# Recurrent layer: score products on quarters of the array, and 32-row corrections issued in turn with the masked values

## The chip, the cores and the metric

The kernel runs on one core of a Trainium2 chip. The metric is the device time of one execution in microseconds (us), from three runs of the kernel before: 1291.12, 1292.26 and 1293.33, with a median of 1292.26.

The engines of the core are named as in the profile: PE is the matrix engine (TensorE), with PEld for its loads of stationary operands; DVE is VectorE, ACT is ScalarE, POOL is GpSimd and SP the engine that issues most DMAs. A matrix product holds one operand in the array (the stationary one, rows by columns) and streams the other through it (the moving one); its result goes to PSUM, from where ACT or DVE copies it on.

## The reference

The model is a two-layer trunk over 512 tokens of width 1024. Layer 0 mixes time with an RWKV-7 recurrence (12 heads of width 64) beside attention into 256 memory tokens; layer 1 uses chunked attention. Each layer ends with a gated feed-forward. All arithmetic is float32. The change touches the recurrence alone:

```python
def step(state, inp):
    r_t, w_t, k_t, v_t, a_t, b_t = inp
    sa = jnp.einsum('bhvk,bhk->bhv', state, a_t)
    state = (state * w_t[:, :, None, :] + sa[..., None] * b_t[:, :, None, :]
             + v_t[..., None] * k_t[:, :, None, :])
    return state, jnp.einsum('bhvk,bhk->bhv', state, r_t)
```

The state of a head is 64 x 64. It decays channel by channel, takes a rank-one correction (a, b) and a rank-one update (v, k), and is read with r. 512 such steps are computed for each head.

## The kernel before, in words

The 512 tokens are cut into 8 chunks of 64 (`NCH`), and two heads share one tile of 128 partitions: head h = 0 lies in partitions 0 to 63 (`HS[0]`), head h = 1 in 64 to 127 (`HS[1]`). So there are six head pairs (`NPAIR`). Inside a chunk the recurrence is solved in closed form: with scores between the tokens of a chunk, the inverse of a unit triangular 64 x 64 matrix, and products with it; only the state passes from chunk to chunk.

Each pair goes through three generators. `prepare` (L1126) makes the projections, the decays and keys, the first scores, and solves the 16 x 16 diagonal blocks of the inverse with DVE and some DMAs. `front` (L1290) computes the score products (L1300), masks them into the tile `ML` on DVE (L1303), transposes keys and values (L1314, L1324, L1326), and builds the 32 x 32 blocks of the inverse from 16 x 16 ones (L1358, L1375). `back` (L1400) completes the inverse to 64 x 64 and runs the chunks.

The change touches these places:

- In `front`, for each half of the chunks (`c4`), two PSUM tiles take the scores, one per head. For each chunk and head one product has a stationary operand of 64 x 128 (two of the three 64-wide slots of `KB`) and 128 moving columns (`AR`). Each head uses its 64 array rows and all 128 array columns.
- In `back`, the first 16 products (L1410) begin the correction that joins two 32-row blocks of the inverse: 32 x 32 stationary, 32 moving columns, at array rows `h*64` to `h*64+32` and array columns `h*64+32` to `h*64+64`. ACT copies them to `X5` (L1414). The second step of the correction (L1424) uses `X5` and finishes `Tt`.
- Between those two, 16 products (L1418) multiply the masked scores with the values: 64 x 64 stationary, 64 moving columns, array rows of the other head (`HS[1 - h]`) and array columns of the own head (`HS[h]`). ACT copies them to `VT[:, 2]` (L1419). Then L1434 applies the inverse to what both steps have made.

The order of the work is written by a planner, `weave` (L87). Each generator yields an estimated cost in nanoseconds, and, as a second number, a time that must pass in the plan before it is asked again; the planner always asks the ready generator with the least share of its total done (`BACK_COST` and its like are these totals). In one stage it weaves `back` of one pair, `front` of the next and `prepare` of the one after (L1577 to L1581); the last stage holds the backs of the last two pairs, one `front` and the memory attention (L1609). These numbers make no semaphores; the build derives the waits from the data and can exchange products whose inputs come ready at other times. The scores, the corrections and the values all take PSUM tiles from one pool of four (`S=4`).

## Time and profile before

| what | us |
|---|---|
| timed runs | 1291.12, 1292.26, 1293.33 |
| median | 1292.26 |
| span of the profiled execution, first to last instruction | 1292.6 |
| PE busy in it | 1260.9 (98%) |
| DVE busy | 1031.7 (80%) |
| ACT busy | 846.4 (65%) |
| DMA packets, bytes | 95581, 192.14 MB |

The profile comes from one execution apart from the timed ones; its span is the time that it gives.

How to read the rows that follow. A row of the timeline gives the start and the duration in us, the engine, the line of the kernel, the operation, the tile written and those read, the stationary shape (rows\*columns), the moving shape, and how many records in sequence were merged (x16); in square brackets stands idle time just before, and what ended it. A float32 product leaves two records. The end of a matrix product is modelled, and products overlap, so durations of PE rows can't be added; the distance between two starts can. In the view of one line, the three durations are the least, the median and the greatest in ns. In the view by windows, each row gives a stretch of the span, the busy time of an engine in it with its count of records, and the granted clock of the matrix engine as a share.

### The profile page before, as it was taken

The numbers are of one execution on the slowest core, as the hardware profiler recorded it, in microseconds if no ns is written. First come the engines' busy times: TensorE is split into PE (matmuls) and PEld (weight loads), VectorE is DVE, ScalarE is ACT, GpSimd is POOL, SyncE is SP. The second block draws the span as 40 slices with busy tenths as digits, with TensorE's granted clock in tenths as the row PEclk, the third lists the DMA queues.
The fourth block names the chain that finished last, engine by engine and source line by source line (L and its number), as shares of the span: only waits on it lengthen the run. The fifth ranks groups of instructions, "written<-read, shape, count | busy, mean of one in ns | idle before, by whom it ended". The sixth has DMA issues, their size and how long they took to land.

```text
span 1292.6 us, 26432 instructions
## 1 busy us (share of the span) xinstructions
PE 1260.9 (98%) x10420; PEld 1083.1 (84%) x10420; DVE 1031.7 (80%) x1956; ACT 846.4 (65%) x1398; POOL 152.7 (12%) x182
## 2 busy tenths in 40 slices
PE   9999999999999999999999999999999999999997
PEld 7887777777789999998888878787789999998886
DVE  7867677765688999998876876658889999998684
ACT  6566767856476777776554676757757777765662
POOL 1000000000001222320220000000002222211200
PEclk9999999999999999999999999999999999999999
DMA  5364444453055988996984322234429989978951
GB/s 204 110 174 106 100 96 89 92 109 96 30 166 126 212 198 198 206 208 172 274 185 122 118 87 82 76 104 123 130 61 212 197 193 211 208 161 262 233 149 66
DMA packets 95581, 192.14 MB, mean 149 GB/s; under 512 B 22112, under 2 KB 30432, under 8 KB 95456
## 3 DMA queue, kind: packets, MB, share of 16 engines
q1 hardware_dynamic: 68592, 129.14, 31.9%
q0 software_dynamic: 26864, 61.31, 27.3%
q8 instruction: 82, 1.34, 0.4%
q14 instruction: 43, 0.35, 0.1%
HBM read 174.20 MB, written 6.29 MB: 140 GB/s over the span
## 4 chain that ended last, share of the span: by engine, by line
PE 62%; DVE 15%; ACT 8%; DMA 8%; issue 6%; SPq 0%; POOL 0%; ACTq 0%; DVEq 0%; POOLq 0%
PE psf L434 8%; PE psf L698 7%; PE psd L245 6%; PE psd L241 5%; PE psd L242 5%; DMA wlv<-in_ffn_in_dram 4%; PE psf L436 4%; PE psf L703 4%; PE psd L698 3%; ACT whi L499 2%; DMA wraw<-in_ffn_in_dram 2%; PE psd L703 2%; DVE raw L486 1%; PE pss L1817 1%; DVE wlo L504 1%
## 5 line engine op out<-in xcount | busy, mean ns | idle before, releaser
L499 ACT CAST whi<-raw 128x1024 fp32r<-128x1024 f32 (+1 forms) x168 | 153.3, 942 | 62.3 <-PE psf L434 29.5
L434 PE MATMUL psf<-th,whi 128*128 128x256 f32 x672 | 161.4, 278 | 2.5 <-ACT tmp L553 1.9
L434 PE MATMUL psf<-tl,whi 128*128 128x256 f32 x672 | 161.1, 276 | 0.0
L195 ACT CAST whi<-wraw 128x1024 fp32r<-128x1024 f32 x84 | 87.6, 1048 | 78.3 <-PE psd L242 37.4
L434 PEld LDWEIGHTS psf<-th,whi 128*128 128x128 f32 x672 | 125.8, 188 | 3.9 <-ACT tmp L553 2.9
L434 PEld LDWEIGHTS psf<-tl,whi 128*128 128x128 f32 x672 | 126.0, 188 | 0.0
L504 DVE TENSOR_TENSOR wlo<-raw,whi 128x1024 fp32r<-128x1024 f32 (+1 forms) x108 | 109.3, 1012 | 9.1 <-ACT whi L499 8.9
L241 PE MATMUL psd<-r1h,whi 128*128 128x512 f32 x264 | 107.4, 408 | 0.0
L242 PE MATMUL psd<-r1l,whi 128*128 128x512 f32 x264 | 105.0, 398 | 0.0
L203 DVE TENSOR_TENSOR wlo<-wraw,whi 128x1024 fp32r<-128x1024 f32 x65 | 79.2, 1219 | 22.3 <-ACT whi L195 20.4
L688 ACT CAST whi<-raw 128x1024 fp32r<-128x1024 f32 (+1 forms) x52 | 49.6, 954 | 59.9 <-PE psf L698 33.1
L689 DVE TENSOR_TENSOR wlo<-raw,whi 128x1024 fp32r<-128x1024 f32 (+1 forms) x52 | 56.5, 1097 | 38.9 <-ACT whi L688 31.5
L436 PE MATMUL psf<-th,wlo 128*128 128x256 f32 x504 | 78.0, 276 | 0.0
L245 PE MATMUL psd<-r1h,wlo 128*128 128x512 f32 x264 | 74.3, 403 | 0.6 <-DMA wlo<-in_ffn_in_dram 0.4
L471 POOL DMA_DIRECT2D wlv<-in_ffn_in_dram x40 | 60.7, 1516 | 59.5 <-DVE tmp L572 59.1
L436 PEld LDWEIGHTS psf<-th,wlo 128*128 128x128 f32 x504 | 66.8, 188 | 0.0
L434 PE MATMUL psf<-r2h,whi 128*128 128x256 f32 x252 | 60.9, 278 | 0.7 <-ACT whi L499 0.7
L434 PE MATMUL psf<-r1h,whi 128*128 128x256 f32 x252 | 60.7, 277 | 0.7 <-ACT whi L499 0.7
L434 PE MATMUL psf<-r2l,whi 128*128 128x256 f32 x252 | 60.7, 277 | 0.0
L434 PE MATMUL psf<-r1l,whi 128*128 128x256 f32 x252 | 60.6, 277 | 0.0
L241 PEld LDWEIGHTS psd<-r1h,whi 128*128 128x128 f32 x264 | 49.6, 188 | 12.0 <-issue 2.1
L525 ACT ACTIVATE tmp<-tmp,vec 128x512 f32<-128x512 f32 x44 | 36.0, 817 | 33.3 <-DVE tmp L512 33.3
(611 smaller groups left out, 3576.8 us busy)
## 6 DMA issues: line engine op xcount, KB each, us to landing
raw<-in_ffn_in_dram SPq DMA_DIRECT2D x42, 512.0 KB, 5.2
raw<-in_ffn_in_dram SPq DMA_DIRECT2D x84, 256.0 KB, 5.5
wlv<-in_ffn_in_dram POOLq DMA_DIRECT2D x40, 512.0 KB, 8.6
raw<-in_ffn_out_dram SPq DMA_DIRECT2D x30, 512.0 KB, 6.2
raw<-in_ffn_out_dram POOLq DMA_DIRECT2D x24, 512.0 KB, 8.4
wraw<-in_wA_dram SPq DMA_DIRECT2D x20, 512.0 KB, 4.1
wraw<-in_w_out_dram SPq DMA_DIRECT2D x16, 512.0 KB, 4.1
wraw<-in_ffn_outp_dram SPq DMA_DIRECT2D x16, 512.0 KB, 4.5
```

What stands on the lines that cost most here:

```text
L195: high = lambda: pin(SC.copy(hi[:, :n], raw))
L203: pin(V.tensor_tensor(lo[:, :n], raw, hi[:, :n], op=ALU.subtract))
L241: PE.matmul(ps, wh[:, j * P:(j + 1) * P], ah, start=start and n == 0, stop=False)
L242: dense_at[0] = PE.matmul(ps, wh[:, j * P:(j + 1) * P], al, start=False, stop=False)
L245: dense_at[0] = PE.matmul(ps, wl[:, j * P:(j + 1) * P], act(k)[0], start=False, stop=stop and n == len(ks) - 1)
L434: PE.matmul(ps, wh[:, o + k * P:o + k * P + P], x[k][n], start=k == n == 0, stop=False)
L436: PE.matmul(ps, wl[:, ol + k * P:ol + k * P + P], x[k][0], start=False, stop=k == 3)
L471: GP.dma_start(self.low[:].rearrange("p (a s) -> p a s", a=2), self.second, accum_op=ALU.add)
L499: keep(SC.copy(hi[:, :n], self.pair(what) if n > S else self.raw[:, what]))
L504: keep(V.tensor_tensor(lo[:, :n], self.pair(what) if n > S else self.raw[:, what], hi[:, :n], op=ALU.subtract))
L698: PE.matmul(ps[:], a[:, k0 + i, ts], hi[:, i * S:i * S + S], start=bool(first) and (first is True or t in first) and a is act[0] and i == ...
L703: PE.matmul(ps[:], act[0][:, k0 + i, ts], lo[:, i * S:i * S + S], start=False, stop=bool(last) and t in last and i == n - 1)
```

## The change

In `front`, each score product with a 64 x 128 stationary operand becomes two with 64 x 64. The four products of a chunk sit in the four quarters of the array: rows of head h, columns of half n, in the order (0,0), (1,1), (0,1), (1,0). The moving operand and the results stay what they were.

In `back`, the corrections and the values were two blocks, each with a yield of its own. They become one: for each chunk the two corrections and then the two value products. The values have a second PSUM tile, `pz`, taken at the same time. All copies on ACT stand behind the whole block. The two yields (650 and `MC`, which is 1280) become one of `MC` with a wait of 400, and `BACK_COST` loses 650.

```diff
     U = [(c, h, HS[h], HS[1 - h]) for c in range(NCH) for h in range(2)]
+    QUADS = ((0, 0), (1, 1), (0, 1), (1, 0))
     MC = 16 * 80
...
-                for h in range(2):
-                    PE.matmul(ps[h][:, c], KB[HS[h], cc, 1 - h:3 - h].rearrange("p s t -> p (s t)"),
+                for h, n in QUADS:
+                    PE.matmul(ps[h][HS[n], c], KB[HS[h], cc, 1 - h + n],
                               AR[HS[h], cc].rearrange("p s t -> p (s t)"), start=True, stop=True)
...
-        ps = ups()
-        for c, h, ap, vp in U:
-            lo, hi_ = slice(h * 64, h * 64 + 32), slice(h * 64 + 32, h * 64 + 64)
-            PE.matmul(ps[hi_, c, 0:32], ML[lo, h, c, 32:64], Tl[lo, c], start=True, stop=True,
-                      tile_position=(h * 64, h * 64 + 32))
+        ps, pz = ups(), ups()
+        for c in range(NCH):
+            for h in range(2):
+                lo, hi_ = slice(h * 64, h * 64 + 32), slice(h * 64 + 32, h * 64 + 64)
+                PE.matmul(ps[hi_, c, 0:32], ML[lo, h, c, 32:64], Tl[lo, c], start=True, stop=True,
+                          tile_position=(h * 64, h * 64 + 32))
+            for h in range(2):
+                PE.matmul(pz[HS[h], c], ML[HS[1 - h], h, c, 0:64], VT[HS[1 - h], h, c], start=True, stop=True)
         for h in range(2):
             hi_ = slice(h * 64 + 32, h * 64 + 64)
             SC.copy(X5[hi_], ps[hi_, :, 0:32])
-        yield 650
-        ps = ups()
-        for c, h, ap, vp in U:
-            PE.matmul(ps[ap, c], ML[vp, h, c, 0:64], VT[vp, h, c], start=True, stop=True)
-        SC.copy(VT[:, 2], ps[:])
-        yield MC
+        SC.copy(VT[:, 2], pz[:])
+        yield MC, 400
...
-    BACK_COST = 2 * 650 + 2 * MC + 4 * 1100 + 1700 + 6 * 150 + 7 * 150 + 700 + 1080
+    BACK_COST = 650 + 2 * MC + 4 * 1100 + 1700 + 6 * 150 + 7 * 150 + 700 + 1080
```

## The prediction

> **What bounds the kernel now.** I read the page first (engine shares, the chain), then the stage in which the changed lines run, then the TensorE timeline around them.

> ```profile
> span 1292.6 us, 26432 instructions
> PE 1260.9 (98%) x10420; PEld 1083.1 (84%) x10420; DVE 1031.7 (80%) x1956; ACT 846.4 (65%) x1398; POOL 152.7 (12%) x182
> ...
> PE 62%; DVE 15%; ACT 8%; DMA 8%; issue 6%; SPq 0%; POOL 0%; ACTq 0%; DVEq 0%; POOLq 0%
> ```

> The changed lines run from 81 us (first scores) to 317 us (last corrections). Busy time of PE in the windows with the `back` pieces:

> ```profile
> core 0: us, PE busy (x), PEclk, DMA share, GB/s
> 105.00:147.00 42.00, 40.21 (x624) 1.00 0.44 96
> ...
> 306.00:330.00 24.00, 23.81 (x458) 1.00 0.10 31
> sum 225.00, PE 218.74; mean PE 36.46
> ```

> PE is busy 218.74 of 225 us at the full clock. While one head pair's recurrence runs, the dense projections of the next pair fill in, so what PE does longer comes out at the end almost in full. I therefore price everything in PE time, from start to start, because the modelled durations overlap. One whole set of the changed sections, and the number of records:

> ```profile
> 288.63 0.69 PE L1410 MATMUL pss<-Tl,ML 32*32 32x32 f32 x32
> 289.25 1.16 PE L1300 MATMUL pss<-AR,KB 64*128 64x128 f32 x16
> 290.34 1.15 PE L1418 MATMUL pss<-VT,ML 64*64 64x64 f32 x32
> 291.42 0.48 PE L1300 MATMUL pss<-AR,KB 64*128 64x128 f32 x2
> ```
> ```profile
> L1410 PE MATMUL pss<-Tl,ML x160: 191/191/212, 112.3 to 289.1; 32*32 32x32 f32 x160
> L1410 PE MATMUL pss<-AR,ML x32: 191/191/212, 314.3 to 314.8; 32*32 32x32 f32 x32
> ```
> ```profile
> L1300 PE MATMUL pss<-AR,KB x192: 272/272/373, 81.3 to 293.3; 64*128 64x128 f32 x192
> ```

> Each fp32 product leaves two records, so 192 records of L1410 are 16 corrections in each of six backs, and 192 of L1300 are 8 score products in each of twelve half sections. From the starts: corrections 289.25 - 288.63 = 0.62 us, a score half 290.34 - 289.25 = 1.09 us, the masked values 291.42 - 290.34 = 1.08 us.

> These rows also show what happens where the shape of the stationary operand changes. Each section starts 0.07 us before the modelled end of the one ahead of it (288.63 + 0.69 = 289.32 against 289.25; 290.41 against 290.34; 291.49 against 291.42). Where the shape stays, nothing of the kind is seen:

> ```profile
> 215.25 0.23 PE L1326 MATMUL pss<-cst,v 64*64 64x64 f32 x2
> 215.26 0.27 PE L1445 MATMUL pss<-ML,W 64*64 64x128 f32 x1
> ```

> Here another line's product starts 0.01 us after a product that lasts 0.23 us. So the array empties when the tile shape changes and only then.

> **The price of one change of shape.** Two short sections give it.

> ```profile
> 112.28 0.24 PE L1410 MATMUL pss<-Tl,ML 32*32 32x32 f32 x2
> 112.46 0.49 PE L1300 MATMUL pss<-AR,KB 64*128 64x128 f32 x2
> 112.87 0.69 PE L1410 MATMUL pss<-Tl,ML 32*32 32x32 f32 x30
> ```
> ```profile
> 314.00 0.33 PE L1467 MATMUL psl<-W,MQ 64*64 64x64 f32 x4
> 314.27 0.69 PE L1410 MATMUL pss<-AR,ML 32*32 32x32 f32 x32
> ```

> A section with a single correction takes 112.46 - 112.28 = 0.18 us, one with 16 (two quarters at a time, so eight times as long in work) 0.62 us: 0.44/14 = 0.031 us for each of its 2 or 16 passes, and 0.12 us fixed. A section with one 64x64 product in each of two quarters, as L1467 is, takes 0.27 us, one with eight in each 1.08 us: 0.81/14 = 0.058 us a pass and 0.15 us fixed. The fixed part is the emptying and the slower first pass.

> **The change part by part.**

> Corrections in turn with values. Per chunk the new loop issues two 32x32 corrections, then two 64x64 products, so PE goes through eight sections of each kind where it had one. The work stays; the fixed parts come seven times more: 7 x (0.12 + 0.15) = 1.90 us a back (8 x 0.45 = 3.60 instead of 0.62 + 1.08 = 1.70). Six backs: +11.4 us. The open point is whether the shapes drain each other even where they use different quarters: correction h sits in the quarter (rows h, columns h), value product h in (rows 1-h, columns h). The trace never has this pair. Its nearest row is the 112.87 one above: the score product at 112.46 is the first of half h = 0, in array rows 0 to 63; of the 30 correction records behind it 16 belong to half 1, in rows 64 to 95, and none started before 112.87, 0.08 us before that product's modelled end. Their input was there:

> ```profile
> 111.39 0.89 DVE L1405 STREAM_TRANSPOSE Tl<-Tt 32x256 f32<-32x256 f32 x2
> ```

> Both transposes had ended at 112.28. So disjoint rows don't spare the wait (the columns were shared), and I take the full price; the other bound is that corrections vanish under the values, -0.62 us a back. [...]

> Shapes that now match. After the last value product the 64x64 scores follow with no change of shape in five backs (L1300 stood behind L1410 in each, as at 289.25): one fixed part less, 5 x 0.15 = -0.75 us. A second score half stands directly ahead of L1434, also 64x64, in three:

> ```profile
> 165.80 1.16 PE L1300 MATMUL pss<-AR,KB 64*128 64x128 f32 x16
> 166.89 1.96 PE L1434 MATMUL pss<-VT,Tt 64*64 64x128 f32 x32
> 168.78 0.50 PE L242 MATMUL psd<-r1l,whi 128*128 128x512 f32 x1
> ```

> 3 x 0.15 = -0.45 us, if the order stays.

> Scores by quarters. The number of products doubles, each with half the columns of weights and the same 128 moving columns. Two rows bound it:

> ```profile
> 300.00 1.09 PE L1445 MATMUL pss<-ML,W 64*64 64x128 f32 x16
> 301.02 0.50 PE L241 MATMUL psd<-r1h,whi 128*128 128x512 f32 x1
> ```
> ```profile
> 91.25 0.27 PE L1324 MATMUL pss<-cst,AR 64*64 64x64 f32 x2
> 91.27 0.28 PE L1326 MATMUL pss<-cst,v 64*64 64x64 f32 x2
> ...
> 92.35 0.50 PE L241 MATMUL psd<-r1h,whi 128*128 128x512 f32 x1
> ```

> Eight products of the new shape in two quarters take 1.02 us (L1445). Four quarters cost hardly more than two: L1324 and L1326 put 64 records of 64 columns into 92.35 - 91.25 = 1.10 us, where L1418's 32 in two quarters took 1.08. So 1.04 us a half instead of 1.09: 12 x -0.05 = -0.6 us. Bounds: nothing gained, or the quarters not overlapping at all, as 16 products two at a time do in L1434 (168.78 - 166.89 = 1.89 us): +0.8 us a half. The rows are nearest to the first. The masking on DVE (L1303) and all copies keep count and size; no DMA is added.

> What waits move. Two PSUM tiles of the four in that pool are now taken together, and the copies of the corrections start only when all 16 are done:

> ```profile
> 113.60 0.74 ACT L1414 COPY X<-pss 32x256 f32<-32x256 f32 x2 [0.24 <-PE pss L1410]
> ...
> 116.94 0.58 ACT L1419 COPY VT<-pss 128x512 f32<-128x512 f32 x1
> ```

> That is 1.3 us of ACT copies behind the section, ahead of L1424, which needs the first 0.74. The scores (1.04) and the dense products that the plan puts between cover it; without them each back would lose 0.74 us. Against that, PE waits near these places today:

> ```profile
> 119.87 0.29 PE L1434 MATMUL pss<-VT,Tt 64*64 64x128 f32 x1 [0.63 <-ACT Tt L1428]
> ...
> 164.09 1.15 PE L1418 MATMUL pss<-VT,ML 64*64 64x64 f32 x32 [0.65 <-DVE ML L1303]
> ...
> 201.58 1.56 PE L1300 MATMUL pss<-AR,KB 64*128 64x128 f32 x16
> ...
> 240.75 1.71 PE L1300 MATMUL pss<-AR,KB 64*128 64x128 f32 x16
> ```

> 0.63, 0.65 and the two stretched score halves (1.56 and 1.71 against 1.16, 0.40 and 0.55) make 2.2 us, and a slower section ahead gives the other engines time to catch up. I let half of it go: -1.1 us. The plan itself (one yield of 650 less, a wait of 400 more, both numbers of the planner and no semaphores) reorders a few dense products; I take 0, between -2.2 (all those waits gone) and one wait like 0.65 more in each of six stages, +3.9.

> Sum: 11.4 - 0.75 - 0.45 - 0.6 - 1.1 = +8.5 us. The profiled execution's span, 1292.6, is 0.3 above the median of 1292.26 and within the runs (1291.12 to 1293.33); I add to the median: **1300.8 us**.

> **The rivals.**

> A, the forecast: every chunk drains twice. From 8.5 with the bounds of the waits (-1.1 to +3.9, and these seldom in full): 1297.5 to 1304.

> B, faster: products in wholly separate quarters don't drain each other, so the corrections run under the values. Place: the new loop; it decides if a correction and a value product of different shape overlap at all. It gains 6 x 0.62 = 3.7, and the -1.8 of the other parts: about 1286.8. For it: same-shape products in four quarters do run together (L1324 with L1326). Against it: every change of shape quoted drains, also across rows. [...]

> C, no change that can be told: the order that the build finally gives PE groups the two kinds, since products are taken as their inputs come ready (the lone score product at 112.46 slipped in between that way). With few alternations left only the -1.8 us remains: 1290.5. Against it: in the other backs the corrections stand in one block, as written.

> D, the change doesn't do what it says for the scores: quarters with 128 moving columns don't overlap. 12 x 0.8 = 9.6 in place of -0.6, on top of A: 1311. L1324 and L1326 speak against it.

> **How the numbers follow.** A 0.66, B 0.22, C 0.08, D 0.04. A's own range is 1297.5 to 1304; to leave out no more than 2 in 10 the range goes down over C to about the middle of B's cases, 1287 to 1304.5. This kernel's measurement can tell about 0.2% (2.6 us) from no change. Faster: nearly all of B, 0.20. Within: C, a B that hides little, 0.12. Slower: A and D less a small tail, 0.68.

> **What would show it.** Right: in the timeline the corrections and values stand in eight alternating groups, x4 each, about 0.45 us a chunk and 3.6 us a back, each starting some 0.07 us before the modelled end of the one ahead; score halves of 32 records take about 1.04 us. B would show correction records starting within a value product's duration, and the two kinds through in about 1.1 us. C would show long blocks of one kind. D would show a score half near 1.9 us. The forecast fails if a back's section is under 2 us, or if the stage's PE wait falls by more than the 2.2 us counted.

## The result, and the profile after

The changed kernel takes 1309.64 us in the median of four executions, against 1292.61 for the kernel before on the same chip: a ratio of 1.013 (95% interval 1.0114 to 1.0146), 17.0 us slower. One of the four fell in a slower state (1327.99 us), as did one execution of a kernel further down (6233.08 us, with 256 instructions added), and the ratios leave both out. The forecast was 1300.8, within 1287 to 1304.5. The direction was right, the size half of what came, and the time lies outside the range. The profiled execution took 1309.91 us, with a span of 1308.1, 15.5 over that of before; the four places below are taken from it. Its page begins so, with the last line from the chain of waits:

```profile
span 1308.1 us, 26821 instructions
PE 1271.3 (97%) x10612; PEld 1089.8 (83%) x10612; DVE 1032.4 (79%) x1956; ACT 847.5 (65%) x1398; POOL 153.1 (12%) x182
...
PE 68%; DVE 13%; ACT 8%; issue 6%; DMA 5%; SPq 0%; POOL 0%; ACTq 0%; DVEq 0%; POOLq 0%
```

TensorE is busy 10.4 us longer and has 192 records more, 389 instructions more in all; the shares tell little else.

**The new loop.** The timeline of TensorE in the kernel after, one whole back from its first correction, cut in its middle, and below it the corrections of the last back (start, duration, line, tile written and read, stationary and moving shape, records):

```profile
160.11 0.25 PE L1412 MATMUL pss<-Tl,ML 32*32 32x32 f32 x4
160.29 0.33 PE L1415 MATMUL pss<-VT,ML 64*64 64x64 f32 x4
160.55 0.25 PE L1412 MATMUL pss<-Tl,ML 32*32 32x32 f32 x4
160.73 0.33 PE L1415 MATMUL pss<-VT,ML 64*64 64x64 f32 x4
...
163.20 0.25 PE L1412 MATMUL pss<-Tl,ML 32*32 32x32 f32 x4
163.38 0.27 PE L1415 MATMUL pss<-VT,ML 64*64 64x64 f32 x2
163.40 0.33 PE L1301 MATMUL pss<-AR,KB 64*64 64x128 f32 x2
163.49 0.23 PE L1415 MATMUL pss<-VT,ML 64*64 64x64 f32 x2
163.55 1.04 PE L1301 MATMUL pss<-AR,KB 64*64 64x128 f32 x30
164.52 0.51 PE L1141 MATMUL pss<-zw,wah 128*128 128x512 f32 x1
...
329.15 0.69 PE L1412 MATMUL pss<-AR,ML 32*32 32x32 f32 x32
```

The eight pairs stand as forecast, 0.44 us each, and every section starts 0.07 us before the modelled end of the one ahead (160.11 + 0.25 = 160.36 against 160.29). From 160.11 to 163.40 one back takes 3.29 us, where the two blocks of before took 1.70. That is 1.59 us more in each of five backs, +8.0 us. The sixth, at 329.15, stands in one block: there the build put all 32 correction records together. The quarter scores follow the values without the 0.07 us step (163.40 lies inside the values that run from 163.38), and a half takes 164.52 - 163.40 = 1.12 us, one value product that it overlaps included.

**A stop in the midst of a burst.** The same view, where 64 products of 16 x 16 stand in a row; first the kernel before, then after:

```profile
307.16 0.69 PE L1375 MATMUL pss<-Y,Tn 16*16 16x16 f32 x64
```
```profile
317.27 0.60 PE L1376 MATMUL pss<-Y,Tn 16*16 16x16 f32 x54
321.01 0.25 PE L1376 MATMUL pss<-Y,Tn 16*16 16x16 f32 x10 [3.14 <-issue]
```

The burst breaks after 54 records for 3.14 us. "issue" says that TensorE waited for nothing that the profile shows.

**The clock.** Windows of the kernel before (first fence) and after (second), with the busy times of TensorE, its weight loads, DVE, ACT and POOL, then the granted clock, the DMA share and GB/s:

```profile
45.00:55.00 10.00, 9.52 (x61) 8.77 (x60) 9.55 (x35) 4.60 (x6) 0.00 (x0) 0.83 0.41 123
```
```profile
245.00:256.00 11.00, 11.00 (x107) 8.13 (x107) 5.23 (x17) 5.98 (x11) 0.86 (x1) 0.71 0.43 97
316.00:326.00 10.00, 6.86 (x132) 5.00 (x121) 3.93 (x8) 4.96 (x12) 0.00 (x0) 0.83 0.36 134
420.00:430.00 10.00, 7.75 (x54) 7.56 (x53) 7.41 (x13) 5.32 (x8) 3.00 (x3) 0.83 0.74 178
```

The granted clock was either full or half (1.00 or 0.50) in both traces, as narrower windows of the kernel after show (TensorE alone, then the same columns):

```profile
246.20:249.50 3.30, 3.30 (x67) 1.00 0.89 216
249.60:256.30 6.70, 6.70 (x34) 0.50 0.25 50
```

So 0.83 in 10 us is 3.4 us at half clock, or 1.7 us of lost work; 0.71 in 11 us is 6.4 us and 3.2 lost. Before has one such stretch in its body, after has these three: 6.6 us lost against 1.7, so +4.9. The first begins at 249.6 us, where an alternating section has just ended (245.60 to 248.88); the second, at 321.3, follows the stop of 3.14 us; the third, at 423.7, follows the late weights of the next place.

**The first feed-forward layer.** Timelines of TensorE and ACT where its first weights are used, before and then after:

```profile
405.02 0.63 ACT L476 ACTIVATE wlo<-raw 128x512 fp32r<-128x512 f32 x1 [0.88 <-DMA raw<-in_ffn_in_dram]
405.96 0.38 PE L434 MATMUL psf<-th,whi 128*128 128x256 f32 x1 [0.19 <-ACT tmp L553]
```
```profile
422.45 0.63 ACT L476 ACTIVATE wlo<-raw 128x512 fp32r<-128x512 f32 x1 [2.91 <-DMA raw<-in_ffn_in_dram]
423.40 0.39 PE L434 MATMUL psf<-th,whi 128*128 128x256 f32 x1 [2.25 <-ACT tmp L553]
```

ACT waits 2.91 instead of 0.88 us for the raw weights, and TensorE 2.25 instead of 0.19 behind it: +2.1 us, for a transfer that the change doesn't touch.

Together: 8.0 (loop) + 3.1 (stop) + 4.9 (clock) + 2.1 (late weights) = 18.1 us. The span grew by 15.5; the 2.6 less are about the 1.8 that the forecast took off for matching shapes and quarters, and 0.8 that I can't assign. So the longer loop accounts for half. Of the other half, the first half-clock stretch (3.2 us) lies right behind the changed loop; the stop, the late weights and the two stretches behind them are in places that the change's own lines don't touch. The experiments are about that half.

### The profile page after: what moved, and what is told of

Read it like the earlier page. It is cut to its first block, busy times and chain, and to the rows that moved or that the text cites. A ratio compares the mean times of both kernels' runs of the same rounds, so it can differ in the third digit from the quotient of the medians.

```text
span 1308.1 us, 26821 instructions
## 1 busy us (share of the span) xinstructions
PE 1271.3 (97%) x10612; PEld 1089.8 (83%) x10612; DVE 1032.4 (79%) x1956; ACT 847.5 (65%) x1398; POOL 153.1 (12%) x182
## 4 chain that ended last, share of the span: by engine, by line
PE 68%; DVE 13%; ACT 8%; issue 6%; DMA 5%; SPq 0%; POOL 0%; ACTq 0%; DVEq 0%; POOLq 0%
PE psf L434 10%; PE psf L698 7%; PE psd L245 6%; PE psd L241 6%; PE psd L242 5%; PE psf L436 5%; PE psf L703 4%; PE psd L698 3%; DMA wraw<-in_ffn_in_dram 2%; PE psd L703 2%; DVE raw L486 1%; DMA wlv<-in_ffn_in_dram 1%; ACT whi L499 1%; PE pss L1817 1%; DVE wlo L504 1%
## 5 line engine op out<-in xcount | busy, mean ns | idle before, releaser
L241 PE MATMUL psd<-r1h,whi 128*128 128x512 f32 x264 | 108.4, 411 | 0.0
L242 PE MATMUL psd<-r1l,whi 128*128 128x512 f32 x264 | 105.5, 401 | 0.0
L241 PEld LDWEIGHTS psd<-r1h,whi 128*128 128x128 f32 x264 | 49.9, 189 | 12.6 <-issue 2.7
L245 PEld LDWEIGHTS psd<-r1h,wlo 128*128 128x128 f32 x264 | 47.6, 190 | 12.6 <-DMA wlo<-in_ffn_in_dram 1.6
```

Source lines behind the costliest of these rows:

```text
L241: PE.matmul(ps, wh[:, j * P:(j + 1) * P], ah, start=start and n == 0, stop=False)
L242: dense_at[0] = PE.matmul(ps, wh[:, j * P:(j + 1) * P], al, start=False, stop=False)
L245: dense_at[0] = PE.matmul(ps, wl[:, j * P:(j + 1) * P], act(k)[0], start=False, stop=stop and n == len(ks) - 1)
```

## The experiments

All times are medians, each compared with runs of the kernel before on the same chip (1291.4 to 1292.6). "Clock" is (1 - mean granted clock) x span, the median of the runs: the time lost to the half clock, its stretch at the very end included. The kernel before has 2.6 us of it. The executions of a changed kernel spread more than those of before (1289.5 to 1295.8 us over all chips): those of the scores alone run from 1297.2 to 1304.4. A trace is one execution, so what is read from it is compared with the difference between spans.

| kernel | us | ratio to before (95%) | clock, us |
|---|---|---|---|
| after | 1309.6 | 1.0130 (1.0114 to 1.0146) | 9.1 |
| scores by quarters alone | 1299.3 | 1.0067 (1.0050 to 1.0083) | 6.5 |
| joined and in turn, old scores | 1312.2 | 1.0162 (1.0149 to 1.0176) | 13.8 |
| joined, in two blocks, old scores | 1293.2 | 1.0011 (0.9999 to 1.0024) | 2.6 |
| joined, in two blocks, quarters | 1303.2 | 1.0087 (1.0066 to 1.0107) | 8.5 |
| after, in turn by two chunks | 1302.8 | 1.0081 (1.0053 to 1.0109) | 7.2 |
| after, corrections as 64x64 | 1305.6 | 1.0111 (1.0096 to 1.0125) | 9.1 |

### The two halves of the change, each alone

The scores by quarters alone: the first hunk of the diff and nothing else.

```diff
-                for h in range(2):
-                    PE.matmul(ps[h][:, c], KB[HS[h], cc, 1 - h:3 - h]...,
+                for h, n in QUADS:
+                    PE.matmul(ps[h][HS[n], c], KB[HS[h], cc, 1 - h + n],
```

> Only the score products go to quarters; the back is that of the kernel before. Drain theory (the loss comes from the corrections alternating with the values, and what follows from that): 1292, a score half at 1.03 instead of 1.09 us, so at most 1 us under before. Rival, instruction supply (the 192 further score records alone make PE wait for its instructions): 1295 to 1296, with a wait of about 3 us put down to issue on a PE row of the layer.

Measured: 1299.27 us, +7.7. Both expectations missed, and this trace has a stop of 1.0 us at "issue" where the rival wanted about 3. The start of the feed-forward layer holds most of the loss. Timeline of ACT there:

```profile
410.82 0.63 ACT L476 ACTIVATE wlo<-raw 128x512 fp32r<-128x512 f32 x1 [4.39 <-DMA raw<-in_ffn_in_dram]
```

4.39 instead of 0.88 us, 3.5 of them new, and behind it the clock is halved (windows, columns as above):

```profile
408.00:420.00 12.00, 8.30 (x50) 8.24 (x50) 7.77 (x13) 5.55 (x9) 3.01 (x3) 0.72 0.61 135
```

That is 0.28 x 12 = 3.4 us at most, since TensorE idles in part of it; with the wait, up to 6.9 of the 7.8 us between this trace's span (1300.4) and that of before (1292.6).

The second half alone: the joined loop of the change with the scores as they were.

> Only the back is changed, alternation, yields and the two PSUM tiles; the scores are 64x128 as before. Drain theory: five backs at about 3.3 us instead of 1.7, so 1301 from that alone, and 1304 to 1310 with half-clock windows as in the changed kernel. Instruction supply: PE has as many products as before, so no long wait for issue and about 3 us less than the changed kernel, 1306.

Measured: 1312.24 us, +20.6, more than the whole change and above both expectations. The two halves therefore don't add: 7.7 + 20.6 against 17.0.

### In blocks, and by two chunks

The joined piece of the kernel after, but all 16 corrections and then all 16 values (written here in short; the run has it as one group of eight chunks):

```diff
         for c in range(NCH):
             for h in range(2):
...
                 PE.matmul(ps[hi_, c, 0:32], ML[lo, h, c, 32:64], Tl[lo, c], ...)
+        for c in range(NCH):
             for h in range(2):
                 PE.matmul(pz[HS[h], c], ML[HS[1 - h], h, c, 0:64], VT[HS[1 - h], h, c], ...)
```

> The changed kernel, but all 16 corrections stand ahead of all 16 values, still in one piece with its two PSUM tiles, its one yield and its costs; scores by quarters. Drain theory: the whole loss goes, 1290 to 1293, no more half-clock windows in the layer than before. Rival, the plan (the merged yield, the two PSUM tiles taken together and the order that follows cost what the drains don't explain, about 7 us): 1298 to 1300.

Measured: 1303.19 us, 6.4 less than after, but above both expectations: the theory that the whole loss would go is refuted. The same blocks with the scores as before:

> The kernel before with only the two pieces of the back joined, all sixteen corrections first and then all sixteen values, and the scores as before; computation unchanged. Theory (drains cost only where the kinds alternate; joining alone changes the order a little): 1292 to 1298 us, and 14 to 18 us below the same kernel with the kinds in turn (1312.2). Rival (joining the pieces itself is dear, by its waits and by what it moves in the order): 1302 us or more.

Measured: 1293.24 us, a ratio of 1.0011 (0.9999 to 1.0024): joining costs nothing that can be told. Its timeline, one back:

```profile
160.39 0.69 PE L1413 MATMUL pss<-Tl,ML 32*32 32x32 f32 x32
161.02 1.15 PE L1417 MATMUL pss<-VT,ML 64*64 64x64 f32 x32
162.09 1.16 PE L1301 MATMUL pss<-AR,KB 64*128 64x128 f32 x16
```

162.09 - 160.39 = 1.70 us, as in the kernel before. So what stays in the blocks with quarters (1303.2) comes with the quarters. Turning the kinds by chunk adds 19.0 us to this kernel (1312.2 - 1293.2), a little more than the 14 to 18 expected, of which five backs of 1.6 us are 8.0 and the lost clock 13.8 - 2.6 = 11.2. These two terms, 19.2 us, are the whole of it. Windows of the kernel in blocks, then of the one in turn, both with the old scores:

```profile
190.00:230.00 40.00, 38.79 (x613) 29.92 (x612) 27.46 (x82) 29.60 (x60) 2.75 (x3) 1.00 0.37 81
230.00:270.00 40.00, 39.38 (x630) 29.78 (x628) 29.90 (x87) 29.76 (x59) 2.49 (x3) 1.00 0.44 93
```
```profile
190.00:230.00 40.00, 37.95 (x532) 28.71 (x530) 22.47 (x63) 27.25 (x56) 1.72 (x2) 0.87 0.32 71
230.00:270.00 40.00, 39.55 (x481) 29.63 (x480) 25.44 (x71) 24.43 (x50) 1.72 (x2) 0.87 0.31 69
```

A granted 0.87 over 80 us is 10.4 us lost in these two windows alone, with TensorE booked as busy as in the other kernel.

In turn by two chunks, four corrections and four values at a time, quarters kept:

> The kernel after with the kinds in turn by two chunks and not by one: four corrections, four values, four times over, so half as many changes of tile shape (8 a back in place of 16); computation unchanged. Theory (each change of shape costs about 0.1 us by a drain): the rows of both kinds 4 us less than in the kernel after over the layer, and a time half way between all in blocks (1303.2) and one by one (1309.6), 1305 to 1308 us. Rival (what costs the time is the sparse stretch that halves the clock, not the drains): within 1.5 us of one or of the other.

Measured: 1302.81 us, no more than the blocks with quarters (1303.19). Its timeline:

```profile
161.31 0.31 PE L1413 MATMUL pss<-Tl,ML 32*32 32x32 f32 x8
161.55 0.45 PE L1417 MATMUL pss<-VT,ML 64*64 64x64 f32 x8
161.93 0.31 PE L1413 MATMUL pss<-Tl,ML 32*32 32x32 f32 x8
```

A pair takes 0.62 us, the four of a back 2.5, between the 1.70 of the blocks and the 3.29 of one by one: the drains follow their count. The median doesn't: it lies below the theory's 1305 to 1308 and within the rival's 1.5 us of the blocks. But the executions run from 1298.2 to 1311.9 us and the interval of the ratio reaches 1306.7 us, so this run decides between neither. Part of the half dose fell where TensorE would have waited anyway, for the masked scores (waits view, blocks with quarters and then by two chunks: us, times, longest):

```profile
PE pss L1325 <- DVE ML L1304: 2.1, 3, 1.0
```
```profile
PE pss L1325 <- DVE ML L1304: 1.3, 3, 0.6
```

That is 0.8 us of 4 (0.8 a back in five); whether the rest is in the time is open.

### One shape for both kinds

The corrections as 64x64 products with the unused rows zeroed on POOL, in turn with the values as in the change: the same turns, no change of shape.

```diff
+        for lo in (slice(32, 64), slice(96, 128)):
+            GP.memset(Tl[lo], 0.0)
...
-                PE.matmul(ps[hi_, c, 0:32], ML[lo, h, c, 32:64], Tl[lo, c], ..., tile_position=...)
+                PE.matmul(ps[HS[h], c, 0:32], ML[HS[h], h, c, 0:64], Tl[HS[h], c], ...)
```

> The changed kernel, but each correction uses the whole 64x64 block of the masked scores as its stationary operand and a moving operand whose other 32 rows are zeroed by POOL, so corrections and values alternate in one shape, one per array quarter. Drain theory: the block of both takes about 1.1 us instead of 3.3 (changed kernel) and 1.7 (before): 1287 to 1290. If alternating itself, and not the change of shape, cost the time, the block stays near 3 us and the kernel at 1305 or more. Plan rival: about 7 us above the drain theory's figure, 1294 to 1297.

Measured: 1305.6 us, far above the drain theory's time and just in the range of the second theory, but that one's block of 3 us isn't there. The drain theory's mechanism shows at once in the timeline of a back:

```profile
160.91 0.25 PE L1413 MATMUL pss<-Tl,ML 64*64 64x32 f32 x2
160.92 0.27 PE L1415 MATMUL pss<-VT,ML 64*64 64x64 f32 x2
...
161.86 1.08 PE L1301 MATMUL pss<-AR,KB 64*64 64x128 f32 x32
163.37 0.49 PE L1141 MATMUL pss<-zw,wah 128*128 128x512 f32 x1 [0.42 <-ACT X L1418]
```

Both kinds together take 161.86 - 160.91 = 0.95 us, against 3.29 with two shapes and 1.70 in blocks. Alternating itself is free, the change of shape is what costs. But 2.3 us a back, 11.7 in five, came back as 4.0 us of time: TensorE now reaches waits for the copies (0.42 us on L1418 above), the late weights are later still (4.34 us at L476), a stop of 2.3 us at "issue" is there, and the lost clock stays at 9.1 us.

### The instruction stream

Each fp32 product is two records, each with a weight load, so four instructions: with the quarters' 96 products more, the records of products and the weight loads both went from 10,420 to 10,612. That is 384 instructions, 64 in the `front` of each pair. The profile counts how the instructions come in: the queue whose count fits TensorE's own instructions, in the kernel before,

```profile
q8 instruction: 82, 1.34, 0.4%
```

82 packets of 1.34 MB, so 16 KB each. With 10,420 records of products and as many weight loads that is 254 instructions a packet, 256 with the 132 semaphore ones that the trace has beside. DMA queues of the kernel after, from 306 to 318 us and then from 318 to 320:

```profile
q1 hardware_dynamic: 1867, 1.24, 39.8%
q0 software_dynamic: 144, 0.52, 23.0%
```
```profile
q1 hardware_dynamic: 264, 0.57, 73.8%
q8 instruction: 1, 0.02, 3.0%
```

For 12 us no packet of instructions came, TensorE stopped at 317.9, the next came after 318 (at 318.7 by the trace's record of that packet), and at 321.0 the burst went on.

That such a stop is the end of a block can be counted. The seventeen traces of this text have 21 waits of TensorE put down to "issue". If the TensorE instructions of a trace (products, loads and semaphore ones) are numbered by their starts, the one that ends the wait is number 193 or 194 over a multiple of 256 in all 21, and it starts 2.2 to 2.5 us after the latest packet of that queue began.

So I asked whether the mere position of the blocks costs time, with no product of the layers moved. Two of the six warm-up products at the start were replaced by 34 tiny ones, 128 instructions more:

```diff
-    for _ in range(6):
-        PE.matmul(idle[:, 0:256], zeros[:, 0:P], zeros[:, 0:256], start=True, stop=True)
+    for k_, n_ in [(32, 16)] * 34 + [(P, 256)] * 4:
+        PE.matmul(idle[0:k_, 0:n_], zeros[0:k_, 0:k_], zeros[0:k_, 0:n_], start=True, stop=True)
```

> The kernel before, with two of the six warm-up products at the very start replaced by 34 tiny ones: 128 more PE instructions ahead of everything else, and not one product in another order. The 16 KB blocks in which PE's instructions are fetched (256 of 64 bytes) then end half a block elsewhere, as they do after the 384 more instructions of the quarter scores. Block theory: a PE wait put down to issue of 1 to 3 us appears in the last L1375 group, the first raw load of the feed-forward lands 2 to 4 us late, and the kernel takes 1295 to 1299. Rival (the new products themselves cost the time): 1291 to 1293.

Measured: 1300.31 us, +9.0, a ratio of 1.0076 (1.0057 to 1.0095), a little above what was expected; the six executions run from 1297.4 to 1306.5. The profiled one, the fastest, has 1.7 us of stops at "issue" and waits 1.9 us longer at L476, and the median has 2.6 us more lost clock (5.2); the 2.8 us left of the 9.0 have no place here. I put the same shift ahead of three other kernels.

Scores by quarters alone:

> The scores-only kernel with the same 128 more instructions at the start, so 512 more than before by the end of the layer, two whole blocks. Block theory: both waits go, 1290 to 1293. Rival: it stays at 1299.

Measured: 1299.81 us (1299.27 without the shift).

The kernel after:

> The changed kernel with the same 128 more instructions at the start. Block theory: the issue wait of 3.1 us, the late raw load (2.3 us) and the half-clock window behind each go; what stays is the draining of the alternating shapes and its own half-clock windows: 1300 to 1304. Rival: it stays at 1308 to 1311.

Measured: 1314.65 us (1309.64), with 14.5 us lost to the clock instead of 9.1.

One shape for both kinds:

> The kernel with corrections and values in one shape, with the same 128 more instructions at the start. Block theory: 1293 to 1299, its issue wait (2.3 us) and late raw load (3.7 us) gone. Rival: it stays at 1304 to 1308.

Measured: 1305.0 us (1305.6). The block theory's times missed in all three kernels; the rival, no change, held in two. The shift mends one place and spoils others. The wait at L476 is short in all three (0.91, 0.77 and 0.85 us). But the stops at "issue" don't go: 2.1, 1.4 and 2.3 us instead of 1.0, 3.1 and 2.3, now two or three in each kernel where there was one. The lost clock is 7.1, 14.5 and 12.4 us instead of 6.5, 9.1 and 9.1.

Is it the shift, or the longer start? Two of the warm-up products made 512 columns wide: more work at the start, no instruction more.

> The kernel before with two of its six warm-up products made 512 columns wide: about 1.7 us more work at the start, as in the shifted start, but not one TensorE instruction more, so no block of TensorE instructions begins at another product. The computation is unchanged. Theory (where the instruction blocks fall against the bursts of small products costs the time): the delay is passed on and nothing else, 1292 to 1294 us. Rival (being 1 to 2 us later against the transfers is what costs the time): 1298 to 1302 us, as with the shifted start (1300.3).

Measured: 1291.82 us, a ratio of 0.9992 (0.9984 to 1.0001). As a control this is weak: in its trace the products of the recurrent layer come only 0.1 to 0.3 us later than in the kernel before (from 120 us on), where 128 instructions more had made that 0.6 us. A start that is later by more comes with the 256 below.

Is it that there are more instructions, whatever their position? Three more starts, with 64, 192 and 256 added; 256 is one whole block, so every boundary comes back to the same product.

> The kernel before with two of its six warm-up products replaced by 18 tiny ones: 64 TensorE instructions more at the start, a quarter of a block; nothing else is changed. Theory (position of the blocks): another time than with 128 and than with none, somewhere in 1292 to 1304 us. Rival (the number of added instructions): half way between the kernel before and 128 added, 1295 to 1297 us.

> The kernel before with four of its six warm-up products replaced by 52 tiny ones: 192 TensorE instructions more at the start, three quarters of a block; nothing else is changed. Theory (position of the blocks): 1292 to 1304 us, not above 128 added by the step that 64 added gives. Rival (the number of added instructions): more than 128 added (1300.3), 1302 to 1306 us.

> The kernel before with four of its six warm-up products replaced by 68 tiny ones, so 256 TensorE instructions more at the start, one whole block: every block boundary stays at the same product. Nothing else is changed. Theory (the position of the blocks costs the time): 1291.5 to 1294.5 us, and no loss at the start of the first feed-forward layer (at most 0.3 us between its first and its hundredth product against the kernel before). Rival (the tiny products at the start, or more instructions as such): slower than the start shifted by 128 (1300.3), 1301 to 1308 us.

| instructions added at the start | us | ratio (95%) | executions, us |
|---|---|---|---|
| 64 | 1295.6 | 1.0022 (1.0008 to 1.0035) | 1291.7 to 1300.2 |
| 128 | 1300.3 | 1.0076 (1.0057 to 1.0095) | 1297.4 to 1306.5 |
| 192 | 1298.8 | 1.0044 (1.0031 to 1.0058) | 1296.3 to 1299.6 |
| 256 | 1295.2 | 1.0023 (1.0014 to 1.0031) | 1293.8 to 1296.8, and the 6233.1 named above |

The most added is among the cheapest, so it isn't the number. The run with 64 fits its theory and its rival alike and decides nothing alone. 3.3 us remain at 256, a little more than was expected. In its trace the layers' products come at a constant 2.1 to 2.2 us behind the kernel before, from 177 us to the feed-forward layer at 390, and its waits have no "issue" in the recurrent layer. So a start that is 2.2 us later brings no stops and costs less than 128 instructions with a start that is 0.6 us later. That the later start is what remains is not shown: this trace's span, 1292.1 us, is no longer than that of before. The waits of 128 and of 192 added do have "issue" (waits of TensorE: us in total, times, longest):

```profile
PE pss L1375 <- issue: 1.7, 3, 1.1
```
```profile
PE pss L1375 <- issue: 1.4, 2, 0.9
PE psl L1472 <- issue: 1.3, 1, 1.3
```

The start of the feed-forward layer divides all seventeen traces the same way. Where the instructions added ahead of it are 128 over a multiple of 256 (128 or 384: the shifted start, the scores alone, both kernels in groups with quarters, the one with one shape, the split scores below, and after), ACT's wait at L476 is 2.80 to 4.45 us. In the ten others (0, 64, 192, 256 or 512 added) it is 0.77 to 1.01. Two rows, of 128 added and of the kernel after with 128 more, so 512:

```profile
408.84 0.63 ACT L476 ACTIVATE wlo<-raw 128x512 fp32r<-128x512 f32 x1 [2.80 <-DMA raw<-in_ffn_in_dram]
```
```profile
421.81 0.63 ACT L476 ACTIVATE wlo<-raw 128x512 fp32r<-128x512 f32 x1 [0.77 <-DMA raw<-in_ffn_in_dram]
```

In all seven traces with the long wait TensorE's instruction queue fetches a block 0.7 to 1.4 us ahead of the first packet of that raw transfer (400.6 and 401.8 with 128 added, 413.9 and 415.3 in the kernel after); in none of the others does one fall there. That the position decides is shown. Whether the fetch makes the transfer late, and how, is not.

### As many instructions without quarters

Every score product of before cut into two by columns, 64 each, the stationary shape kept: 384 instructions more, no quarters.

```diff
-                    PE.matmul(ps[h][:, c], KB[...], AR[HS[h], cc]..., ...)
+                    for n in range(2):
+                        PE.matmul(ps[h][:, c, n * 64:n * 64 + 64], KB[...], AR[HS[h], cc, n], ...)
```

> The kernel before with every score product of 64x128 stationary and 128 columns made as two products with the same stationary shape and 64 columns each: as many more TensorE instructions as the quarters bring, but no quarters; nothing else is changed. Theory (more TensorE instructions in the bursts, and their blocks shifted, are what the scores by quarters cost beside their own rows): 1296 to 1302 us, like the quarters (1299.3). Rival (the quarters themselves cost it): 1291.5 to 1294 us.

Measured: 1308.71 us, above both expectations, since the cut has a price of its own that I had not counted:

```profile
297.81 2.05 PE L1301 MATMUL pss<-AR,KB 64*128 64x64 f32 x32
```

2.05 us a half where 16 records took 1.16, 0.9 more in twelve halves: 10.7 of the 16.1 us. The 5.4 left are near the 7.7 of the quarters, and this kernel too has the late weights (4.45 us at L476). So about what the quarters cost can come from as many instructions without quarters. The run does not prove it: the price of the cut is worked out from one row, and the number of instructions isn't parted from their position here.

No kernel beats the one before. The joined blocks with old scores equal it.

## Why the prediction was right or wrong

**The price of a change of shape.** Right in kind: each change drains (every section of the turns starts 0.07 us before the modelled end of the one ahead), also between wholly separate quarters, which no row before had shown; the kernel with one shape proves it (0.95 us a back). The term was +11.4 and measured 8.0 (1.59 us in place of 1.90 a back, and five backs in place of six). Rival C, grouping by the build, came true for one back of six, which the forecast had not mixed in.

**Rival B** (separate quarters don't drain each other, 1286.8) is refuted by the same rows: no correction starts earlier than 0.07 us before the modelled end of the values ahead of it, and a back takes 3.29 us, not about 1.1. The row from which I chose the full price, a score product with shared columns, was the right one.

**Matching shapes and quarters.** -1.8 us was forecast. The quarter scores follow the values with no drain, and a half takes about 1.1 us, as two quarters suggested. Rival D (1.9 us a half) is out.

**"What waits move"** is the step that failed. I took -1.1 us for waits that a slower section would absorb, and 0 for the plan, within -2.2 to +3.9. Measured in the profiled execution are +3.1 for the stop at L1376, +4.9 for the half clock and +2.1 for the late weights: +10.1 where the term's upper end was +3.9. I looked for waits at semaphores between the engines next to the changed lines. The three that came are of other kinds: one in TensorE's own instruction supply, one in its clock, one in a transfer some 90 us later. The clock in part follows from the alternation itself: 3.2 of the +4.9 us stand right behind an alternating section, and with the old scores the lost clock (11.2 us) is more than the longer loop (8.0), yet the prediction priced a change of shape by its drain alone. Two signs were in the profile of before: its stretch at 0.83, and its 82 packets of instructions. "PEclk 1.00" in the windows of the recurrent layer told me that the clock was full there, not that it would stay so; and the number of instructions, which the change raises by 384, I costed only as work. With the +10.1, in place of -1.1, and the loop at 8.0, the sum is 8.0 - 1.8 + 10.1 = 16.3, against 15.5 between the spans, from which these terms are read, and 17.0 between the medians.

**The range** reached 1304.5 because D was the only case above A. The ends of A were also added up wrongly, since the waits' bounds were laid on a sum that already held their -1.1. With +3.9 in place of the -1.1 the sum is 1305.8, still below what was measured. That a kernel whose four executions beside the changed one lie within 2.2 us (1291.12 to 1293.33) can move by 7 to 9 us from where its instructions happen to lie was in none of the cases. In the rows of before there was no number for it; only an experiment that moves nothing but the position could give one.

## What to carry to other kernels

Keep products with different stationary shapes in blocks: turning 32x32 and 64x64 by chunk cost 1.6 us in a back of 1.7, while the same turns in one shape cost nothing. Count the instructions that an edit adds, not only their time, and where an edit moves the time with no row to explain it, add a few idle products at the start as a control: here 128 instructions alone were worth 9 us in the median. A gain or a loss below that spread (64 to 256 added: 3 to 9 us) says little of the edit until the control is run.

## What the runs showed of the hardware

**Half clock with TensorE booked busy.** In the window from 245 to 256 us of the kernel after TensorE is busy 11.00 of 11.00 us and the granted clock is 0.71; in the 3.3 us ahead of the half clock, which an alternating section nearly fills, it is busy throughout (3.30 of 3.30). The same stands behind 7 of the 15 alternating sections in the three traces that have them: one of five in the kernel after, three of five in the same with 128 instructions more at the start, three of five in turn with the old scores. The half-clock stretches, but for the one at the very end, are 3.41 us long in the kernel before (from 49.80 us) and 6.83, 3.41 and 3.41 us in the kernel after (from 249.57, 321.25 and 423.65). In the 3.4 us ahead of the last two, behind the stop and the late weights, TensorE had been busy for 0.3 and 1.2 us; ahead of the one at 249.57, behind the alternating section, for all 3.4. With the old scores the same work in blocks had a granted 1.00 from 190 to 270 us, where that in turn had 0.87 (2.6 against 13.8 us lost over the whole kernel). Alternation isn't the only way there: one more such stretch, at 248.3 us of the kernel with the split scores, follows corrections and split scores in two blocks, without a gap. Why the clock was halved with no idle time booked, and why 8 of the 15 sections kept the full clock, stays open.
